# A second wave of projections made steps of the fill, its first wave evicted from PSUM, and the roots of the norms on ScalarE, in a two-layer hybrid encoder on one core

## The chip, the core and the metric

The kernel runs on one core of one Trainium2 chip. The metric is the time of one execution on the device in microseconds. The engines are TensorE (PE in the profile, PEld its weight loads), VectorE (DVE), ScalarE (ACT), GpSimd (POOL) and SyncE (SP), which here issues nearly all DMAs.

## What is computed

1024 tokens of width 1024 pass through two layers, all in float32. Each layer has four groups of attention heads side by side, then an MLP. The part that the change touches, cut from the reference:

```python
h = rms_norm(x, norm1_g[l])                 # x * rsqrt(mean(x*x) + 1e-6) * g
proj = h @ w_in[l]
(a_cq, a_ckv, a_kr, b_q, b_k, b_v, c_q, c_k, c_v, d_q, d_k, d_v) = split(proj)
y_a = mla_mixer(a_cq, a_ckv, a_kr, ...)     # rms_norm of a_cq (192) and a_ckv (128), then up-projections
y_b = diff_mixer(b_q, b_k, b_v, ...)        # softmax(q1 k1) - lam * softmax(q2 k2), rope on q and k
y_c = swa_mixer(c_q, c_k, c_v, ...)         # window of 128, sink logits
y_d = na_mixer(d_q, d_k, d_v, rpb[l])       # neighbourhood on a 64-wide grid
mix = concat([rms_norm(y_a), y_b, rms_norm(y_c), rms_norm(y_d)])
x = x + mix @ w_out[l]
h = rms_norm(x, norm2_g[l])
x = x + square(relu(h @ w_up[l])) @ w_down[l]
```

After both layers stands one more RMSNorm.

## The kernel before

**Data.** x is held in SBUF channel by channel, 8 tiles of 128 x 1024 tokens. To keep float32 accuracy on TensorE each operand is split into a high and a low part (`split`: ScalarE copies the high part, VectorE or GpSimd subtracts), and each product takes three matmuls (`passes`, L220 to L222: high by high, low by high, high by low). A projection tile is 128 output channels: 8 blocks of the contraction x 3 passes x 2 halves of 512 tokens = 48 matmuls, each half into one PSUM bank.

**Banks.** During attention the eight PSUM banks are named `mm` (2), `tr` (2), `sb` (3) and `pv` (1): projections, transposes, scores, and probabilities times values.

**Start of a layer.** `attention` first runs a wave of three projection tiles (B's first Q, K and V tile: BQ[0], BK[0], BV[0]) through `several` on the six banks sb, sb, sb, tr, tr, pv, interleaved, while the norm of x is computed (`squares`, `rstd_cols`, `spread_here`; the factor 1/rms ends up in `rb`, one row for each token spread over all partitions, and in the cosine and sine tables `tabc` and `tabs`). ScalarE then copies each bank into an SBUF tile `raw` (L449, shown as `p<-sb`, `p<-tr`, `p<-pv`), and VectorE evicts from that copy: for Q and K `ev_rope` (three products with the tables, an add, and the split into a tile `both`, which is stored to DRAM as `qb` or `kb`), for V a product with `rb`, a transpose on TensorE into `tr` and the split (`to_values`, stored as `vb`). A second wave runs the same for BQ[1], BK[1], BV[1] on the same six banks, its additions and subtractions on GpSimd (`self.eng`). `part` tiles have three buffers and `both` tiles two, so an eviction needs the store before last to have landed.

**Attention with fill.** `weave` alternates steps of an attention (`main`) with single steps of a generator of other work (`fill`), by a ratio: with RB = (7, 8) eight steps of fill come for seven of B's attention. LB is the priority lead that the scheduler gives the main steps. During B's attention (`attn_b`: loads of `stack` and `v` tiles from qb, kb, vb; scores in `softmax`, L804; their row maximum on VectorE, L806, which also moves the scores from the bank to SBUF; exponential on ScalarE, L809; the factor `cb` between the two softmaxes, L890 and L891; transposes L840; products with v, L828 and L829) the fill is `proj_latent` and then `proj_d`. `one` is a projection tile of the fill: two halves, each through an `mm` bank and then its eviction. `proj_latent` makes A's latents, stored to DRAM as `lat`, and their norms: sums of squares `sq` of 128x8, then `rsqrt_cols`, `rows_of` (to DRAM, shown as `drows`). During D's attention the fill is `proj_c` and `latent_up`, which loads the latents as `latp`, into buffers that the projections leave, and projects them up (L720 and L220 to L222).

**Roots.** `rsqrt_cols` (L241 to L252) computes 1/sqrt on VectorE: a guess from the bits (L247), then three Newton rounds of three ops (L249, L188, L251). It is called 20 times. The line number L188 is that of the helper `tt`, so all tensor-tensor ops on VectorE and GpSimd show it and are told apart by their tiles. L194 and L198 are in `split`.

**Order.** The scheduler of the tile framework turns all this into one fixed list of instructions for each engine, by a timeline of its own and by the leads. On the chip each engine, and each queue of DMA issues, takes its list strictly in order and waits at semaphores.

## Time and profile before

| | |
|---|---|
| median of 3 runs | 2735.67 us (2726.91 to 2736.3) |
| the profiled execution, its own time | 2728.97 us |
| its span from first to last instruction | 2727.2 us |
| mean granted clock of TensorE | 0.967 |
| TensorE busy | 2553.1 us |
| VectorE, ScalarE, GpSimd busy | 1994.1, 1430.9, 1134.5 us |

A span has two layers. In layer 0, B's first tiles are projected up to 83 us, B's attention runs to 333, D's starts near 333, the last projection ends at 363, the MLP begins near 758; layer 1 begins near 1372. A row of waits names the engine and the line that waited, the releaser, the total in us, the times and the longest. A row of groups has line, engine, operation, tiles out<-in with sizes, the count, busy time and mean ns of one, then the idle time ahead of them with its releaser. A row of a timeline has start and length in us.

### The profile page before, as it was taken

To read this page: it belongs to the slowest core of one execution; us is meant where nothing else is said; L and a number is where in the kernel's file an instruction comes from. 1 tells how busy PE (TensorE), PEld (TensorE's weight loads), DVE (VectorE), ACT (ScalarE), POOL (GpSimd) and SP (SyncE) were. 2 spreads that over 40 slices of the span, in tenths; PEclk is the share of its full clock that TensorE was granted. 3 is DMA by queue.
4 is the path that set the end of the run, shared out by engine and by line. 5 is a ranking of instruction groups with operands and counts; after the bars stand their busy time and mean duration, and the time that the engine had idled before them with its cause. 6 is when DMAs were issued, how large, how long until landed. Compare 5 with 4: busy or idle time off the path is not lost.

```text
span 2727.2 us, 37613 instructions
## 1 busy us (share of the span) xinstructions
PE 2553.1 (94%) x12298; PEld 2110.1 (77%) x12298; DVE 1994.1 (73%) x3544; ACT 1430.9 (52%) x2547; POOL 1134.5 (42%) x754
## 2 busy tenths in 40 slices
PE   8989988899989999999999899889998999999997
PEld 6778876787778887888877688767886788878886
DVE  7787767674966669787567778677749666687786
ACT  4667757563534444444436676576635344444444
POOL 2555642111245554445435556331013455545552
...
GB/s 175 166 105 126 154 280 241 83 93 40 65 130 156 151 160 267 156 138 142 98 133 138 95 134 157 300 215 71 76 70 44 154 159 149 223 222 150 131 100 62
DMA packets 190516, 389.20 MB, mean 143 GB/s; under 512 B 23712, under 2 KB 30832, under 8 KB 190320
## 3 DMA queue, kind: packets, MB, share of 16 engines
q1 hardware_dynamic: 176496, 361.62, 43.0%
...
q14 instruction: 98, 0.80, 0.1%
...
## 4 chain that ended last, share of the span: by engine, by line
PE 70%; DVE 14%; DMA 7%; ACT 4%; issue 3%; SPq 1%; POOL 1%; DVEq 0%; ACTq 0%; POOLq 0%
PE u L220 8%; PE u L222 8%; PE u L221 8%; PE mm L220 5%; PE mm L221 5%; PE mm L222 5%; PE p L220 5%; PE p L221 5%; PE p L222 5%; PE sb L804 3%; PE tr L840 2%; DVE p L806 2%; DVE part L188 2%; PE pv L829 2%; PE pv L828 2%
## 5 line engine op out<-in xcount | busy, mean ns | idle before, releaser
L188 POOL TENSOR_TENSOR wl<-raw,wh 128x512 fp32r<-128x512 f32 x448 | 635.1, 1418 | 705.2 <-ACT wh L194 690.1
L194 ACT ACTIVATE wh<-raw 128x512 fp32r<-128x512 f32 x448 | 281.5, 629 | 579.8 <-PE u L221 315.0
L188 POOL TENSOR_TENSOR wl<-ws,wh 128x512 fp32r<-128x512 f32 (+1 forms) x112 | 148.1, 1325 | 456.9 <-ACT wh L194 426.0
L220 PE MATMUL u<-far,wh 128*128 128x512 f32 x768 | 301.5, 393 | 11.5 <-ACT ev L1237 8.3
L188 DVE TENSOR_TENSOR raw<-raw 128x512 f32<-128x512 f32 x256 | 226.4, 890 | 107.4 <-POOL wl L188 56.9
L222 PE MATMUL u<-far,wl 128*128 128x512 f32 x768 | 300.5, 391 | 1.9 <-POOL wl L188 1.9
L221 PE MATMUL u<-far,wh 128*128 128x512 f32 x768 | 300.3, 391 | 0.0
L188 DVE TENSOR_TENSOR ptl<-tr,pth 128x512 fp32r<-128x512 f32 (+2 forms) x384 | 238.3, 628 | 66.6 <-ACT pth L194 64.9
L809 ACT ACTIVATE p<-p,nm 128x1024 f32<-128x1024 f32 x192 | 220.1, 1147 | 99.8 <-DVE nm L806 98.9
L194 ACT ACTIVATE pth<-tr 128x512 fp32r<-128x512 f32 (+2 forms) x384 | 205.6, 546 | 121.0 <-PE tr L840 64.8
L220 PE MATMUL p<-far,wh 128*128 128x512 f32 x640 | 251.7, 393 | 7.6 <-DVE ev L188 7.6
L222 PE MATMUL p<-far,wl 128*128 128x512 f32 x640 | 250.9, 392 | 1.5 <-POOL wl L188 1.5
L221 PE MATMUL p<-far,wh 128*128 128x512 f32 x640 | 251.0, 392 | 0.0
L804 PE MATMUL sb<-stack 96*128 96x512 f32 x640 | 218.5, 424 | 24.7 <-DVE nm L806 24.0
L188 DVE TENSOR_TENSOR far<-act,far 128x512 fp32r<-128x512 f32 x224 | 208.6, 960 | 14.6 <-ACT far L194 14.6
L188 POOL TENSOR_TENSOR p<-p 128x1024 f32<-128x1024 f32 x64 | 154.3, 2415 | 141.1 <-ACT p L893 125.0
L220 PEld LDWEIGHTS u<-far,wh 128*128 128x128 f32 x768 | 145.4, 189 | 43.6 <-ACT ev L1237 9.2
L222 PEld LDWEIGHTS u<-far,wl 128*128 128x128 f32 x768 | 145.0, 189 | 33.2 <-POOL wl L188 2.7
L220 PE MATMUL mm<-xh,wh 128*128 128x512 f32 x416 | 169.4, 407 | 0.8 <-DVE rows L272 0.2
L806 DVE CUSTOM_DVE_ANT_0 p<-sb,zero,nm 128x512 f32<-128x512 f32 x192 | 142.4, 743 | 36.3 <-PE sb L804 32.8
L221 PEld LDWEIGHTS u<-far,wh 128*128 128x128 f32 x768 | 145.3, 189 | 30.2
L221 PE MATMUL mm<-xl,wh 128*128 128x512 f32 x416 | 166.6, 400 | 0.0
...
## 6 DMA issues: line engine op xcount, KB each, us to landing
act<-acts SPq DMA_DIRECT2D x224, 256.0 KB
raw<-in_w_up SPq DMA_DIRECT2D x128, 256.0 KB
acts<-ev SPq DMA_DIRECT2D x128, 256.0 KB
raw<-in_w_down SPq DMA_DIRECT2D x128, 256.0 KB
...
```

Of the source, the lines that this page charges most:

```text
L188: (eng or self.nc.vector).tensor_tensor(out=out, in0=a, in1=b, op=op)
L194: nc.scalar.activation(hi, src, AF.Copy)
L220: mm(ps, w[0], x[0][:, sl], start=start, stop=False)
L221: mm(ps, w[0], x[1][:, sl], start=False, stop=False)
L222: mm(ps, w[1], x[0][:, sl], start=False, stop=stop)
L804: self.nc.tensor.matmul(ps, q[:, qt * P:(qt + 1) * P], k[:, sl], start=i == 0, stop=i == len(passes) - 1)
L806: self.nc.vector.tensor_tensor_reduce(out=p[:, sl], in0=ps, in1=self.zero[:, 0:1].bitcast(F).broadcast_to([P, 512]), scale=-scale, scalar= ...
L809: self.nc.scalar.activation(p, p, AF.Exp, bias=nm[:, 1:2], scale=-1.0, accum_out=z)
L828: nc.tensor.matmul(out, v[:, kt], h[:, sl], start=kt == 0, stop=False)
L829: nc.tensor.matmul(out, v[:, kt], lo[:, sl], start=False, stop=kt == 7)
L840: nc.tensor.transpose(t[:, k * 256 + i * P:k * 256 + (i + 1) * P], p[:, (j * 2 + k) * P:(j * 2 + k + 1) * P], self.ident)
```

## The change

1. Only the first wave is left (`FIRST`). Its six banks are evicted by VectorE straight from PSUM; ScalarE's copies L449 go. V's transposes of the first tile go to `tr`, as before.
2. BQ[1], BK[1], BV[1] become `proj_b`, three `one` tiles on the two `mm` banks ahead of the rest of the fill of B's attention, evicted from PSUM, with additions and splits on GpSimd as for the second wave before; V's transposes of this tile now use `mm`. RB goes from (7, 8) to (3, 4). Per pass this makes 512 instead of 416 matmuls into `mm`, 48 instead of 96 into `sb`, 32 instead of 64 into `tr` and 16 instead of 32 into `pv`.
3. `rsqrt_cols` takes sums of squares, from PSUM where they are made there, and computes exp(-0.5 ln(ss / count + eps)) on ScalarE, its square on ScalarE, and one Newton round: `ms` and two ops on VectorE.
4. The norms of the two latents are joined in one call of 128x16 (18 calls in all), after one product that scales the sum of the 128-wide latent by 192/128; their rows are stored together. `spread` reads rows that lie one behind the other.
5. L891 becomes a TENSOR_SCALAR with two columns as factors. A load of ScalarE's function table for logarithm and exponential stands at the start of the program; the list of ScalarE has one such load before and one after.

ScalarE's list goes from 2325 to 2355 rows, VectorE's from 3546 to 3381, SyncE's from 1337 to 1335; GpSimd keeps 759.

```diff
-    def rsqrt_cols(self, ms):
+    def rsqrt_cols(self, ss, count):
+
         nc = self.nc
-        n = ms.shape[1]
-        r = self.cp.tile([P, n], F, tag="rs_r", name="rs_r")
-        t = self.cp.tile([P, n], F, tag="rs_t", name="rs_t")
-        nc.vector.tensor_scalar(r.bitcast(I32), ms.bitcast(I32), -0.5, 1597463007.0, ALU.mult, ALU.add)
-        for _ in range(3):
-            nc.vector.scalar_tensor_tensor(out=t, in0=r, scalar=-0.5, in1=r, op0=ALU.mult, op1=ALU.mult)
-            self.tt(t, t, ms)
-            nc.vector.scalar_tensor_tensor(out=r, in0=t, scalar=1.5, in1=r, op0=ALU.add, op1=ALU.mult)
+        n = ss.shape[1]
+        tile = lambda tag: self.cp.tile([P, n], F, tag=tag, name=tag)
+        ms, r, t = tile("ms"), tile("rs_r"), tile("rs_t")
+        nc.scalar.activation(r, ss, AF.Ln, scale=1.0 / count, bias=self.eps)
+        nc.vector.tensor_scalar(ms, ss, -0.5 / count, -0.5 * EPS, ALU.mult, ALU.add)
+        nc.scalar.activation(r, r, AF.Exp, scale=-0.5)
+        nc.scalar.activation(t, r, AF.Square)
+        self.tt(t, t, ms)
+        nc.vector.scalar_tensor_tensor(out=r, in0=t, scalar=1.5, in1=r, op0=ALU.add, op1=ALU.mult)
         return r
...
         for t in range(n):
-            nc.tensor.matmul(ps[:, t * g:(t + 1) * g], sq[:, t * P:(t + 1) * P], rhs, start=True, stop=True)
-        ms = self.cp.tile([P, n * g], F, tag="ms", name="ms")
-        nc.vector.tensor_scalar(ms, ps, 1.0 / count, EPS, ALU.mult, ALU.add)
-        return self.rsqrt_cols(ms)
+            nc.tensor.matmul(ps.rearrange("p (g t) -> p t g", g=g)[:, t], sq[:, t * P:(t + 1) * P], rhs,
+                             start=True, stop=True)
+        return self.rsqrt_cols(ps, count)
     def rows_of(self, col, grid=False):
...
     def spread(self, dst, rows, j=0, g=1):
-        src = rows.rearrange("(t g) p -> g t p", g=g)[j]
-        n = dst.shape[0]
-        self.load(dst.rearrange("p (t q) -> p t q", t=8), src.partition_broadcast(n))
+        src = rows.rearrange("(g t) p -> g (t p)", g=g)[j]
+        self.load(dst, src.partition_broadcast(dst.shape[0]))
     def spread_here(self, dst, col):
...
         ka, va = dr([2, 2, P, S], "kan"), dr([4, P, 8, P], "va")
-        def evacs_b(t):
+        def evacs_b(t, tag="mm"):
             return [self.ev_rope(tabs, qb[:, t]), self.ev_rope(tabs, kb[:, t]),
-                    self.ev_plain(rb, self.to_values(vb[2 * t:2 * t + 2], "tr"))]
+                    self.ev_plain(rb, self.to_values(vb[2 * t:2 * t + 2], tag))]
         def one(t, xs, ev):
...
                     xs = self.normed(self.g1[:, l], lambda n: self.big_tile(R, n))
-                    def wave():
-                        return [(self.bank(a), self.bank(b)) for a, b in (("sb", "sb"), ("sb", "tr"), ("tr", "pv"))]
-
-                    banks = wave()
+                    banks = [(self.bank(a), self.bank(b)) for a, b in (("sb", "sb"), ("sb", "tr"), ("tr", "pv"))]
                     self.several(first, xs, banks, ahead)
                     acc = self.squares(self.x, self.ap, "p", self.NP)
                     with tc.high_priority(offset=200):
                         self.spread_here(rb, self.rstd_cols(acc, DM, self.ones[:, 0:1]))
                     tabs = self.table("32", rb, nc.vector)
                     self.eng = nc.vector
-                    for t in range(2):
-                        for ev, b in zip(evacs_b(t), banks):
-                            raw = self.ptile()
-                            for n in range(2):
-                                sl = slice(n * 512, n * 512 + 512)
-                                nc.scalar.activation(raw[:, sl], b[n], AF.Copy)
-                                ev(n, raw[:, sl])
-                        if t == 0:
-                            banks = wave()
-                            self.several([w_in(t) for t in self.WAVES[1]], xs, banks)
-                        self.eng = nc.gpsimd
-
-                    fill = chain(self.proj_latent(l, one, xs, rb, tabs, lat, krd, rows), proj_d())
+                    for ev, b in zip(evacs_b(0, "tr"), banks):
+                        for n in range(2):
+                            ev(n, b[n])
+                    self.eng = nc.gpsimd
+
+                    def proj_b():
+                        for t, ev in zip((T_BQ[1], T_BK[1], T_BV[1]), evacs_b(1)):
+                            yield from one(t, xs, ev)
+
+                    fill = chain(proj_b(), self.proj_latent(l, one, xs, rb, tabs, lat, krd, rows), proj_d())
                     self.weave(chain.from_iterable(self.attn_b(l, t, qb, kb, vb, y["b"]) for t in range(2)),
...
     EARLY, RC, RA, LA = 4, (8, 1), (3, 1), 0
-    WAVES = [(T_BQ[t], T_BK[t], T_BV[t]) for t in range(2)]
-    NP, RB, RD, LB, LD = 6, (7, 8), (3, 2), 40, 50
+    FIRST = T_BQ[0], T_BK[0], T_BV[0]
+    NP, RB, RD, LB, LD = 6, (3, 4), (3, 2), 40, 50
     def weave(self, main, fill=iter(()), ratio=(1, 0), lead=0, end=True, every=1):
...
         nc = self.nc
-        squares = [self.col("sq%d" % i, 8) for i in range(3)]
+        cols = self.col("sq", 24)
+        both = cols[:, 0:16]
+        squares = [cols[:, i * 8:i * 8 + 8] for i in (0, 2, 1)]
         for i, t, g in ((0, T_CQ, self.gq[:, l, 0:1]), (2, T_CKV, self.gkv[:, l:l + 1])):
...
         self.tt(q, q, squares[1], ALU.add)
-        for m, count in ((q, 192), (k, 128)):
-            nc.vector.tensor_scalar(m, m, 1.0 / count, EPS, ALU.mult, ALU.add)
-            rows_out.append(self.rows_of(self.rsqrt_cols(m)))
+
+        nc.vector.tensor_scalar(k, k, 192 / 128, None, ALU.mult)
+        rows_out.append(self.rows_of(self.rsqrt_cols(both, 192)))
         yield True
     def latent_up(self, l, lat, rows, qa, ka, va):
         nc, d = self.nc, self.d
         rq, rkv = self.big_tile(F, "rq"), self.big_tile(F, "rkv")
-        self.spread(rq, rows[0])
-        self.spread(rkv, rows[1])
+        self.spread(rq, rows[0], 0, 2)
+        self.spread(rkv, rows[0], 1, 2)
         parts = []
...
                 nc.vector.reciprocal(c, z[1][:, qt:qt + 1])
-                nc.vector.scalar_tensor_tensor(out=c, in0=z[0][:, qt:qt + 1], scalar=self.nlam[:, l:l + 1], in1=c,
-                                               op0=ALU.mult, op1=ALU.mult)
+                nc.vector.tensor_scalar(c, c, z[0][:, qt:qt + 1], self.nlam[:, l:l + 1], ALU.mult, ALU.mult)
                 nc.scalar.activation(ps[1], ps[1], AF.Copy, scale=c)
```

How the lists of the engines move, at the three places that the prediction speaks of.

**TensorE behind the first wave of layer 0.** `xh` and `xl` are the high and low parts of x times the norm's gain, `wh` and `wl` those of a weight block; the first operand named is the bank. Before, behind the first wave, from the second wave on:

```order
L638 MATMUL tr<-ident,part 128x128 x8
L222 MATMUL sb<-xh_177,wl 128x512 x2
L220 MATMUL sb<-xh_181,wh 128x512
L221 MATMUL sb<-xl_182,wh 128x512
L222 MATMUL sb<-xh_181,wl 128x512
L220 MATMUL sb<-xh_181,wh 128x512
L221 MATMUL sb<-xl_182,wh 128x512
L222 MATMUL sb<-xh_181,wl 128x512
```

The changed kernel at the same place:

```order
L224 MATMUL mm<-xh_188,wl 128x512
L222 MATMUL mm<-xh_192,wh 128x512
L223 MATMUL mm<-xl_193,wh 128x512
L224 MATMUL mm<-xh_192,wl 128x512
L636 MATMUL tr<-ident,part 128x128 x8
L222 MATMUL mm<-xh_164,wh 128x512
L223 MATMUL mm<-xl_165,wh 128x512
L224 MATMUL mm<-xh_164,wl 128x512
```

Ahead of V's transposes TensorE now has one tile, BQ[1], in the two mm banks, where six banks were being filled; the next tile needs an mm bank that VectorE has evicted.

**VectorE at the evictions of the first two B tiles of layer 0.** `both<-tr` is the split of V behind its transposes. Before:

```order
L188 TENSOR_TENSOR part<-p,rb 128x512 x2
L188 TENSOR_TENSOR both<-part,both 128x512
L188 TENSOR_TENSOR both<-tr,both 128x8x64 x2
L188 TENSOR_TENSOR part<-p,tabc 128x512
L188 TENSOR_TENSOR part<-p,tabs 64x512 x2
```

The changed kernel:

```order
L190 TENSOR_TENSOR part<-tr,rb 128x512
L190 TENSOR_TENSOR part<-pv,rb 128x512
L190 TENSOR_TENSOR both<-part,both 128x512
L190 TENSOR_TENSOR part<-mm,tabc 128x512
L190 TENSOR_TENSOR part<-mm,tabs 64x512 x2
L190 TENSOR_TENSOR part<-mm,tabc 128x512
L190 TENSOR_TENSOR both<-tr,both 128x8x64
L190 TENSOR_TENSOR part<-mm,tabs 64x512 x2
L190 TENSOR_TENSOR both<-tr,both 128x8x64
L190 TENSOR_TENSOR part<-mm,tabc 128x512
L806 ISA p,nm<-sb,zero 128x512
```

The evictions of BQ[1] stand around V's splits, and the first row maxima of B's scores (L806) follow a little later, between those of BK[1]. On SyncE's list nine loads of `stack` tiles, which wait for K's stores, stand in the changed kernel between the last K store and the store of V's first half; before, one load of a stack stood there.

**VectorE at the roots of the latents of layer 0.** Before, in part:

```order
L688 TENSOR_SCALAR sq_829<-sq_829 128x8
L806 ISA p,nm<-sb,zero,nm 128x512
L806 ISA nm 128x1
L247 TENSOR_SCALAR rs_r<-sq_829 128x8
L247 TENSOR_SCALAR rs_r<-sq_831 128x8
L249 SCALAR_TENSOR_TENSOR rs_t<-rs_r 128x8 x2
L188 TENSOR_TENSOR rs_t<-rs_t,sq_829 128x8
L188 TENSOR_TENSOR rs_t<-rs_t,sq_831 128x8
L251 SCALAR_TENSOR_TENSOR rs_r<-rs_t,rs_r 128x8 x2
L249 SCALAR_TENSOR_TENSOR rs_t<-rs_r 128x8 x2
L198 SCALAR_TENSOR_TENSOR both<-part,par,both 64x512
L188 TENSOR_TENSOR rs_t<-rs_t,sq_829 128x8
```

The changed kernel:

```order
L251 TENSOR_SCALAR ms<-sq 128x16
L806 ISA p,nm<-sb,zero 128x512
L806 ISA nm 128x1
L200 SCALAR_TENSOR_TENSOR both<-part,par,both 64x512
L806 ISA p,nm<-sb,zero,nm 128x512
L806 ISA nm 128x1
L890 RECIPROCAL cb<-z_1123 128x1
L891 TENSOR_SCALAR cb<-cb,z_1122,nlam 128x1
L190 TENSOR_TENSOR rs_t<-rs_t,ms 128x16
L255 SCALAR_TENSOR_TENSOR rs_r<-rs_t,rs_r 128x16
L806 ISA p,nm<-sb,zero 128x512
L806 ISA nm 128x1
```

Two interleaved chains of small ops become one, with row maxima (L806) between its ops. Before B's first scores TensorE's list has 54 us of work at full clock in place of 68, by the counts of rows and the pace of 0.23 us of a matmul.

10 lines of the change are left out of this document (8 added, 2 removed).

## The prediction

> **What bounds the kernel now.** I read the engine shares first, to see whose time the span is.
>
> ```profile
> PE 2553.1 (94%) x12298; PEld 2110.1 (77%) x12298; DVE 1994.1 (73%) x3544; ACT 1430.9 (52%) x2547; POOL 1134.5 (42%) x754
> ```
>
> TensorE is busy for 94% of the span, and the change leaves its list of matmuls all but as it was. So the change can only win what TensorE loses: 6% idle time, and stretches at a lower granted clock. Where these losses lie is read from the table of stages. The first number is the length of the stretch, then come the busy times of PE, PEld, DVE, ACT and POOL, then the granted clock and the DMA share.
>
> ```profile
> 45.80:83.20 37.40, 34.53 (x153) 27.61 (x152) 24.45 (x28) 9.97 (x18) 12.41 (x9) 1.00 0.76 201
> 83.20:106.90 23.70, 19.39 (x71) 15.12 (x70) 21.30 (x36) 13.42 (x22) 14.62 (x10) 0.78 0.73 227
> 106.90:150.80 43.90, 43.00 (x241) 35.92 (x240) 35.09 (x94) 34.78 (x57) 22.53 (x13) 1.00 0.38 109
> 150.80:188.80 38.00, 28.02 (x129) 22.08 (x128) 32.78 (x83) 22.54 (x35) 22.82 (x12) 0.78 0.31 84
> 188.80:363.40 174.60, 173.97 (x963) 148.76 (x962) 128.78 (x340) 126.45 (x216) 96.09 (x56) 1.00 0.55 155
> 363.40:387.30 23.90, 16.30 (x84) 14.03 (x83) 14.05 (x34) 9.90 (x24) 13.28 (x8) 0.86 1.04 291
> 387.30:438.30 51.00, 42.71 (x240) 34.61 (x239) 41.79 (x109) 37.35 (x97) 12.70 (x9) 0.97 0.90 284
> 1417.00:1457.00 40.00, 36.28 (x143) 28.27 (x141) 29.57 (x49) 19.58 (x33) 26.25 (x17) 0.87 0.79 232
> 1482.00:1525.00 43.00, 34.34 (x182) 27.73 (x180) 39.94 (x94) 27.60 (x45) 26.63 (x16) 0.83 0.44 117
> ```
>
> Busy time times granted clock is the work at full clock; the length less that is what a stretch loses. In layer 0 the second wave (45.8 to 83.2) loses 37.4 - 34.5 = 2.9 us, the start of B's attention (83.2 to 106.9) 23.7 - 19.39 x 0.78 = 8.6, the next stretch 0.9, the stretch from 150.8 16.1, the 175 us behind it 0.6. Then the stretch of D's attention with the first latent up-projections (363.4 to 387.3) loses 23.9 - 16.30 x 0.86 = 9.9 and the one after it 9.6. So 28.5 us are lost from the second wave to 188.8, and 19.5 us early in D's attention. Layer 1 repeats this: its two rows lose 40.0 - 36.28 x 0.87 = 8.4 and 43.0 - 34.34 x 0.83 = 14.5. What ends TensorE's idle time is in the tables of waits: first from 30 to 220 us, then from 330 to 400, then from 1380 to 1570.
>
> ```profile
> PE sb L804 <- DVE nm L806: 10.9, 7, 5.0
> ```
>
> ```profile
> PE mm L720 <- DMA latp<-lat: 2.7, 2, 2.2
> PE mm L221 <- DMA latp<-lat: 2.4, 1, 2.4
> PE mm L220 <- DMA latp<-lat: 1.3, 1, 1.3
> ```
>
> ```profile
> PE sb L804 <- DVE nm L806: 10.6, 8, 5.7
> ```
>
> In both layers B's scores wait for VectorE's row maxima (L806), and early in D's attention the latent up-projections wait 6.4 us for a load.
>
> **Part 1: the second wave becomes fill, evicted from PSUM.** Its matmuls stay, only later and in other banks. ScalarE's copies go, and VectorE's operands come from PSUM.
>
> ```profile
> L449 ACT ACTIVATE p<-sb 128x512 f32<-128x512 f32 x12 | 6.9, 590 | 26.0 <-PE sb L222 26.0
> L188 DVE TENSOR_TENSOR part<-p,tabs 64x512 f32<-64x512 f32 x32 | 39.8, 1244 | 2.8 <-POOL part L188 2.4
> L188 DVE TENSOR_TENSOR part<-mm,tabs 64x512 f32<-64x512 f32 (+1 forms) x40 | 27.6, 689 | 0.7
> ```
>
> Per layer 12 copies of about 0.59 us leave ScalarE (7.1 us), and 16 VectorE products with the sine table fall from 1.24 to 0.69 us (8.9 us). That work lies beside TensorE, so it counts only where TensorE waits for it. Against it stands what the second wave covered: TensorE ran 144 matmuls in six banks while VectorE evicted the first wave and while its values made their round trip.
>
> ```profile
> 61.31 0.68 DVE L188 TENSOR_TENSOR both<-part,both 128x512 fp32r<-128x512 f32 x1
> 64.83 0.69 DVE L188 TENSOR_TENSOR both<-tr,both 128x512 fp32r<-128x512 f32 x1 [2.84 <-ACT both L642]
> 68.74 0.69 DVE L188 TENSOR_TENSOR both<-tr,both 128x512 fp32r<-128x512 f32 x1 [3.22 <-ACT both L642]
> ```
>
> ```profile
> L642 ACT ACTIVATE both<-tr 128x512 fp32r<-128x512 f32 x8 | 4.8, 596 | 15.9 <-DMA kb<-both 15.7 <-PE sb L804 0.2
> ```
>
> Here the new wait lies. The split of V into the two `both` buffers waits for the stores of K (15.7 us of ScalarE's waiting over both layers), and VectorE waits behind it, 2.84 and 3.22 us. Afterwards the evictions of BQ[1] and BK[1] are queued behind that split on VectorE, and they alone free the two mm banks. Walking the changed order with the durations above, I find TensorE idle some 8 to 9 us up to the first scores, against 2.9 + 8.6 = 11.5 lost in before by 106.9. The walk can't see the clock or when stores land, so I take a **gain of 0** for the start, between a loss of 8 (a second round of those store waits, 2.84 + 3.22, with some clock lost) and a gain of 8 (nearly all of the 8.6).
>
> **Part 2: B's attention up to 188.8, with the joined latent root.** The worst gap there, on VectorE, GpSimd and TensorE in turn:
>
> ```profile
> 163.87 1.92 DVE L688 TENSOR_SCALAR sq<-sq 128x8 f32<-128x8 f32 x1
> 166.37 1.79 DVE L247 TENSOR_SCALAR rs_r<-sq 128x8 int32<-128x8 int32 x2
> 168.12 2.34 DVE L249 SCALAR_TENSOR_TENSOR rs_t<-rs_r 128x8 f32<-128x8 f32 x2
> 170.42 1.32 DVE L188 TENSOR_TENSOR rs_t<-rs_t,sq 128x8 f32<-128x8 f32 x2
> ```
>
> ```profile
> 163.40 2.35 POOL L188 TENSOR_TENSOR tabc<-tabc,rb 128x1024 f32<-128x1024 f32 x1
> 165.72 2.33 POOL L188 TENSOR_TENSOR tabs<-tabs,rb 128x1024 f32<-128x1024 f32 x1
> 168.02 2.34 POOL L188 TENSOR_TENSOR p<-p 128x1024 f32<-128x1024 f32 x1
> ```
>
> ```profile
> 173.63 0.80 PE L804 MATMUL sb<-stack 96*128 96x512 f32 x1 [4.98 <-DVE nm L806]
> ```
>
> Ops of 8 columns last as long as the GpSimd op beside them: VectorE's ends at 165.79, 168.16 and 170.46 stand within about 0.1 us of GpSimd's 165.75, 168.05 and 170.36. Meanwhile no row maximum is taken, and a score waits 4.98 us for its bank. The change replaces these two roots (two TENSOR_SCALARs ahead, then 10 ops each) by one chain with four VectorE ops and three on ScalarE, spread among the softmax ops, so I expect this gap to go. What is late next: VectorE itself. It is busy 32.78 of these 38 us, and the evictions of the second tile of B, done by 106.9 before, now fall partly into this stretch. Counting rows by durations for the same TensorE work (about 58 us of it), VectorE had 63 us in before with 27 in the last third, and has 66 afterwards, spread evenly. So I take half of the 16.1 us, **8 us per layer**, between -4 (the 3 us of added VectorE work on the path) and 16.
>
> Two small groups of VectorE go with this part.
>
> ```profile
> L891 DVE SCALAR_TENSOR_TENSOR cb<-z,nlam,cb 128x1 f32<-128x1 f32 x64 | 28.6, 447 | 1.2
> L890 DVE RECIPROCAL cb<-z 128x1 f32<-128x1 f32 x64 | 10.2, 159 | 17.6 <-ACT p L809 17.4
> L688 DVE TENSOR_SCALAR sq<-sq 128x8 f32<-128x8 f32 x4 | 4.5, 1134 | 0.1
> ```
>
> L891 becomes a TENSOR_SCALAR. At L890's price it saves 64 x (447 - 159) = 18 us of VectorE; at that of L688, a TENSOR_SCALAR too, it costs 64 x (1134 - 447) = 44 more. It has one column like L890, so I take the saving. Most of it falls where TensorE has no idle time (0.6 us in 175), so it adds nothing to the sum beyond the 8 us; the other end is in the -4.
>
> The Trainium skill, "SBUF — State Buffer", section "Who interferes with whom", says that a VectorE instruction with two SBUF inputs, or one such as tensor_scalar in a two-port mode, shuts out GpSimd or is shut out for a whole instruction, while one with a single SBUF input outside these modes is not. The rows agree for L249 and for the products, 1244 ns from SBUF and 689 from PSUM; by the same rule L891's new form may still be delayed, as L688 is, and the 8 us would be about 0 if all 64 were.
>
> **Part 3: the early part of D's attention.** With the second wave in the fill and the ratio (3,4) in place of (7,8), 192 of 768 projection matmuls are left at B's last score, by the two listings, where 74 of 624 were. D's first score comes after 253 us of TensorE work instead of 281, and 48 instead of 30 of the scores of D and C stand ahead of the first latp matmul; from the release of the buffers of the projections to that matmul lie about 11 us of TensorE work in place of 8.3. That covers 2.7 of the 6.4 us of waiting on latp, and part of the loss of clock (0.86): **5 us per layer**, between -3 (the share of DMA is 1.04 there, and a denser start loads more at once) and 10, which is half of the 19.5.
>
> **Part 4: the other roots.**
>
> ```profile
> PE mm L297 <- DVE rs_r L251: 4.8, 1, 4.8
> ```
>
> ```profile
> 753.46 0.15 DVE L263 TENSOR_SCALAR ms<-mm 128x8 f32<-128x8 f32 x1
> 758.18 0.17 DVE L251 SCALAR_TENSOR_TENSOR rs_r<-rs_t,rs_r 128x8 f32<-128x8 f32 x1
> ```
>
> ```profile
> 2713.68 0.16 DVE L263 TENSOR_SCALAR ms<-u 128x4 f32<-128x4 f32 x1 [1.96 <-PE u L261]
> 2715.65 0.16 DVE L251 SCALAR_TENSOR_TENSOR rs_r<-rs_t,rs_r 128x4 f32<-128x4 f32 x1
> ```
>
> ```profile
> L352 ACT ACTIVATE lam_e<-lam_e 128x2 f32<-128x2 f32 x2 | 0.4, 192 | 1.3 <-DVE lam_e L351 1.3
> ```
>
> Ahead of the MLP the chain from L263 to the last L251 takes 758.35 - 753.46 = 4.9 us with other VectorE ops between, and TensorE waits 4.8. Three ScalarE ops of about 0.19 us and two of VectorE of 0.17, with a few of those others still between, make about 2.9: **2 us** in layer 0, and I take **1.5** for the same chain in layer 1. The chain at the end takes 2715.81 - 2713.68 = 2.1 us, and three of 0.19 plus two of 0.16 with some room for changes of engine make 1.2: **0.9 us**. The bounds of the three are 0 and 6 together. The roots of the sub-norms and group norms lie beside full TensorE stretches: nothing, and 2 us each if uncovered. The functions of the new roots need a table on ScalarE, which is loaded once:
>
> ```profile
> 0.73 1.28 ACT L194 ACT_TABLE_LOAD   x1 [0.73 <-PEq L1479]
> ```
>
> The changed listing holds one load too, so I charge nothing.
>
> **The sum**, against the profiled execution's own 2728.97 us: 2 x (0 + 8 + 5) + 2 + 1.5 + 0.9 = 30.4, so 2698.6. That execution is 6.7 us below the median of the runs shown, 2735.67; with half of this difference added I predict **2702 us**.
>
> **The rivals.**
> - *The start gets slower.* The K stores take long (the DMA share is 0.76 and 0.73 there), and V's first store now stands on SyncE's queue behind nine loads of stacks. VectorE stands in the V split while two full mm banks stop TensorE, where six banks ran on before. Price: the 7.9 us of store waits per layer, in the open for both tiles' `both` pair, and a clock loss like today's first 8.6: some 17 us per layer, 34 in all, less 4 from the roots, so about 2759. It decides if a store lands later than about 9 us after its issue. For it: the 3.22 us waits exist already. Against it: the kernel before lost 8.6 us there too.
> - *Nothing comes of it.* The second wave's 144 matmuls only change places, the gap at 173.63 is taken over by VectorE's evictions, and 175 us of full TensorE show that the fill has no idle time to use. Roots alone: 2728.97 - 4.4 = 2725; with some loss at the start, 2733.
> - *Both stalls vanish.* 8.6 + 16.1 per layer, 10 from D's two stretches and 4.4 from roots: 2728.97 - 63.8 = 2665. For it: the evictions from PSUM escape GpSimd. Against it: VectorE's 66 us of work for 58 of TensorE's.
>
> **How the numbers follow.** The forecast with its own range of 2684 to 2720 has 0.45, the larger gain 0.13, no change 0.20, slower 0.22. About 0.5% (13.7 us) is what a measurement of this kernel can tell from no change: faster is below 2722, slower above 2749. Faster takes the first two, 0.58; the slower rival gives 0.21 to slower, and 0.21 is left within. The range leaves out the lower half of the larger gain and the upper half of the slower case: **2664 to 2758**.
>
> **What would show it.** Right: no score waits over 2 us for L806 near 170 us; L891's mean near 0.16 us; a loss up to the first 82 us of TensorE work like today's; waits on latp near 4 us; about 3 us at the MLP's root. Wrong: waits of the mm banks' matmuls on VectorE of over 4 us between 55 and 80 us with a clock below 0.8 (the slower case), or VectorE near 100% from 130 to 190 us with the score waits as long as before (no change).

## The result, and the profile after

**Same time.** Over 12 runs of each on one chip the changed kernel has a median of 2732.49 us (2723.7 to 2744.56), the kernel before 2732.3 (2725.18 to 2740.56): a ratio of 1.0003 with a 95% interval of 0.9986 to 1.002. Forecast were 2702 us and a range from 2664 to 2758. So the time lies within the range, but the gain of 30 us that was forecast isn't there. The engine shares of the changed kernel hardly differ on TensorE; VectorE has 61 us less.

```profile
PE 2553.6 (94%) x12296; PEld 2110.7 (77%) x12296; DVE 1932.7 (71%) x3379; ACT 1429.7 (52%) x2577; POOL 1129.1 (41%) x754
```

The table of stages, at cuts of the changed kernel itself (the waves' end, the first scores, the latents' root, B's end at 305, the last projection at 372), has length, then busy times of PE, PEld, DVE, ACT, POOL, then clock and DMA share:

```profile
46.10:73.00 26.90, 22.62 (x93) 18.01 (x92) 20.70 (x27) 5.40 (x9) 7.74 (x6) 0.87 0.69 196
73.00:96.50 23.50, 21.34 (x96) 16.32 (x96) 15.83 (x41) 15.40 (x26) 17.32 (x12) 1.00 0.92 282
96.50:152.80 56.30, 53.31 (x292) 43.49 (x291) 42.19 (x117) 43.53 (x71) 24.08 (x12) 0.97 0.33 105
152.80:183.20 30.40, 27.97 (x137) 22.45 (x135) 25.62 (x58) 22.86 (x39) 22.28 (x13) 0.89 0.37 105
183.20:305.20 122.00, 117.51 (x644) 100.41 (x644) 91.85 (x242) 88.01 (x142) 65.80 (x36) 0.97 0.40 120
305.20:371.60 66.40, 64.76 (x348) 55.31 (x347) 36.20 (x88) 35.54 (x82) 30.75 (x22) 1.00 0.74 202
371.60:400.00 28.40, 22.38 (x117) 18.96 (x116) 17.89 (x40) 13.54 (x35) 11.85 (x8) 0.88 1.01 280
400.00:441.90 41.90, 28.07 (x144) 22.59 (x142) 27.00 (x69) 24.04 (x61) 11.61 (x8) 0.84 0.93 290
```

With busy time times clock as work, the first four stretches lose 7.2 (26.9 - 22.62 x 0.87), 2.2, 4.6 and 5.5 us, together 19.5 in place of the 28.5 before. That looks like a gain of 9 us, but the cut at 183.2 us falls into the middle of the wait for the latents' root: from 183.2 to 188.7 TensorE is busy for 3.11 us at a clock of 0.50, which loses another 3.9 us. So about 23 us stand against 28.5, and the count of matmuls below leaves still less of the gain in layer 0. B's second half loses 122 - 117.51 x 0.97 = 8.0, those 3.9 among them, where the 175 us from 188.8 lost 0.6 before. The stretch from 400 loses 41.9 - 28.07 x 0.84 = 18.3; that is the largest loss of the table.

The waits of TensorE name the place. First those for VectorE at the start of B, layer 0 from 30 to 220 us and layer 1 from 1372 to 1560; then, from 365 to 490 us and from 1715 to 1845, a wait that stood at 3.2 and 3.4 us before:

```profile
PE sb L804 <- DVE nm L806: 6.9, 9, 2.4
PE mm L222 <- DVE part L190: 2.7, 2, 1.8
PE tr L636 <- DVE part L190: 2.4, 1, 2.4
```

```profile
PE sb L804 <- DVE nm L806: 3.7, 7, 1.0
PE mm L222 <- DVE part L190: 2.2, 1, 2.2
...
PE tr L636 <- DVE part L190: 1.8, 1, 1.8
```

```profile
PE pv L1026 <- DVE y L190: 11.8, 5, 7.9
```

```profile
PE pv L1026 <- DVE y L190: 5.0, 4, 2.1
```

Scores wait for VectorE's row maxima 6.9 and 3.7 us in place of 10.9 and 10.4 in the same stretches, and in place of the single gap of 4.98 us the longest is 2.4, at 185.6 us, still beside the latents' root. The waits for VectorE's evictions (`part`) have grown, from 2.0 and 2.9 us to 5.1 and 4.0. What is new behind B is the wait of `pv` for `y`, up to 7.9 us at once. The timeline of the changed kernel shows its chain, engine by engine:

```profile
417.59 1.33 ACT L199 ACTIVATE mixh<-rz,g_sub 128x512 fp32r<-128x512 f32 x2 [4.33 <-DMA rz<-yb]
419.01 0.34 SPq L169 DMA_DIRECT2D yb<-y  x1
424.12 0.68 DVE L190 TENSOR_TENSOR y<-pv,pvt 64x512 f32<-64x512 f32 x1 [3.93 <-DMA yb<-y]
424.95 0.77 PE L1026 MATMUL pv<-zero 128*128 128x512 f32 x1 [7.88 <-DVE y L190]
```

B's last output `yb` is stored at 419 us; only when that store has landed is its `y` buffer free (there are two), VectorE can evict a pv bank into it, and TensorE gets the bank. VectorE's wait for the store is 3.9 of the 7.9 us; ahead of it VectorE stands in B's tail (`mixl`), whose load ScalarE waits for. In the kernel before the same store was issued earlier, although B ended 28 us later there:

```profile
406.22 0.34 SPq L167 DMA_DIRECT2D yb<-y  x1
```

The roots became what was expected of them. Ahead of the first MLP and at the end of the program, the first and the last op of each chain:

```profile
758.83 0.27 ACT L250 ACTIVATE rs_r<-mm,eps 128x8 f32<-128x8 f32 x1 [1.20 <-PE mm L265]
761.92 0.17 DVE L255 SCALAR_TENSOR_TENSOR rs_r<-rs_t,rs_r 128x8 f32<-128x8 f32 x1
...
2715.82 0.26 ACT L250 ACTIVATE rs_r<-u,eps 128x4 f32<-128x4 f32 x1 [1.12 <-PE u L265]
2716.79 0.16 DVE L255 SCALAR_TENSOR_TENSOR rs_r<-rs_t,rs_r 128x4 f32<-128x4 f32 x1
```

They take 762.09 - 758.83 = 3.3 us in place of 4.9, and 1.1 in place of 2.1.

**Times at equal work.** Each kernel has the same matmuls in another order, so times of milestones can't be compared directly. For the table below each matmul record counts as the pace of its size (from the kernel before's trace, such that 20% of the intervals between its start and the next start are shorter: 0.226 us for 512 columns, 0.118 for 256, 0.175 for 384, 0.029 for a transpose of 128); summed up, this is work, about 2263 us in each kernel. A cell says how many us a kernel gained (-) or lost (+) against the kernel before's first trace while it did that piece of work. A0 ends at 140 us of work (194 us in the kernel before), B0 at 240 (308.5), D0 at 380 (about 536), M0 at the end of layer 0's MLP (about 1356); A1, B1, D1 are the same pieces of layer 1, M1 the rest. Each row is one profiled execution; its sum lies within 12 us of what the medians give, so the columns, not the sums, are what they are for.

```
                        A0     B0     D0     M0     A1     B1     D1     M1    sum
before, again         -1.1   -0.0   +0.1   -1.6   -2.7   +0.1   +0.6   -1.7   -6.4
changed               -0.1   +4.1   +1.0   -0.1   -6.0   -0.8   +7.2   -4.1   +1.1
changed, again        -4.1   +3.9   +5.8   -1.6   -3.4   -0.7   +7.7   -4.6   +2.8
e1  move alone        +5.6   +1.9   -2.5   +0.1   +2.1   -2.5   +5.7   +0.3  +11.0
e2  roots alone       -6.8   +1.6   -6.9   -0.4  -11.3   +0.6   +4.6   -3.5  -22.1
e3  RB (1,2)         -10.4   +3.0   -0.2   -0.3  -14.2   +0.0   +9.1   -2.7  -15.3
e4  waves from PSUM   -3.0   +2.3   -5.6   +0.3   -5.7   +0.0   +8.6   -0.1   -3.1
e5  RB (1,1)          -0.1  +19.0   -0.3   -1.0   -3.0  +16.7   +4.3   -2.6  +32.9
e6  roots, e4        -11.7   +5.2   -7.4   -1.3  -15.3   -0.9   +7.8   -3.5  -27.1
e7  L891 alone        -1.7   +1.5   +4.6   -1.1   -2.6   -0.3  +14.0   +1.2  +15.5
e8  more DMA in D     +1.0   -0.1   -0.4   -0.9   -2.9   +0.1  +10.1   -1.2   +5.7
e11 RB (1,3)         -14.7  +10.6   +9.1   -0.5  -17.5   +7.0  +14.5   -3.6   +5.2
e12 roots, old L891   -3.4   +0.7   +1.8   -1.7   -4.8   -2.4   +8.7   -3.7   -4.6
e17 move, RB (1,2)    -0.6  +12.9   -6.4   +1.3   -5.4   +3.4  +17.2   +3.8  +26.2
e18 faster tails      -5.3   +4.1   -8.9   -0.3   -3.0   -2.7   -3.2   -2.7  -22.1
```

The second trace of each of the two kernels shows what a cell is worth: the same lists differ by up to 4.0 us, and once by 4.8, in D0. So -1.1 in A0 and -2.7 in A1 are what the kernel before gains on itself, and the changed kernel's -0.1 and -4.1, -6.0 and -3.4 are hardly more than that. B0 begins at 194 and D0 at 308.5 us of the kernel before, so D0 holds the last 25 us of B's attention. In D1 every changed program of the table but e18 loses 4 to 17 us, those without the moved wave too; a part of D1's +7 is then not particular to the move, and why the kernel before is so good there is open. Some of the profiled executions lie well off their kernel's median: e18's is 8.4 us below it, e3's 6.6 below, e11's 6.1 above.

### The profile page after: what moved, and what is told of

It is laid out like the page before. It is cut to its first block, busy times and chain, and to the rows that moved or that the text cites. A ratio compares the mean times of both kernels' runs of the same rounds, so it can differ in the third digit from the quotient of the medians.

```text
span 2728.4 us, 37493 instructions
## 1 busy us (share of the span) xinstructions
PE 2553.6 (94%) x12296; PEld 2110.7 (77%) x12296; DVE 1932.7 (71%) x3379; ACT 1429.7 (52%) x2577; POOL 1129.1 (41%) x754
## 5 line engine op out<-in xcount | busy, mean ns | idle before, releaser
L222 PE MATMUL mm<-xh,wh 128*128 128x512 f32 x512 | 207.4, 405 | 8.7 <-DVE part L190 7.2
L223 PE MATMUL mm<-xl,wh 128*128 128x512 f32 x512 | 204.8, 400 | 0.0
L224 PE MATMUL mm<-xh,wl 128*128 128x512 f32 x512 | 204.6, 400 | 0.0
L222 PEld LDWEIGHTS u<-far,wh 128*128 128x128 f32 x768 | 145.6, 190 | 43.0 <-ACT ev L1236 6.8
L840 PE MATMUL tr<-ident,p 128*128 128x128 f32 x1024 | 160.6, 277 | 9.8 <-POOL p L190 5.0
```

Of the source, the lines that this page charges most:

```text
L222: mm(ps, w[0], x[0][:, sl], start=start, stop=False)
L223: mm(ps, w[0], x[1][:, sl], start=False, stop=False)
L224: mm(ps, w[1], x[0][:, sl], start=False, stop=stop)
L840: nc.tensor.transpose(t[:, k * 256 + i * P:k * 256 + (i + 1) * P], p[:, (j * 2 + k) * P:(j * 2 + k + 1) * P], self.ident)
```

## The experiments

The theory (T, with F and Y as its parts) is that the parts do win time early in a layer, and that it is given back in B's second half, where the ratio leaves too little fill, and behind B, where something comes later. The rivals are that nothing was won at all (R), that the granted clock takes back what idle time goes (C), or that the DMA engines are the limit behind the projections (D). Ratios are to the kernel before on the same chip, with 95% intervals.

**e1 and e2: the two parts alone.** e1 is the changed kernel with the old `rsqrt_cols`, `rstd_cols`, `spread`, latent norms and L891; e2 is the kernel before with the new ones.

```diff
# e1, against the changed kernel: old rsqrt_cols, and so on
-        nc.scalar.activation(r, ss, AF.Ln, scale=1.0 / count, bias=self.eps)
+        for _ in range(3):
...
# e2, against the kernel before: the same lines the other way round, the two waves kept
```

> The changed kernel with the old roots, the old latent norms, the old way of spreading rows and the old L891: the moved wave alone. Theory T (the fill wins some 10 us per layer up to 190 us of a layer, but its 192 instead of 74 left-over projections end later, and D's and C's stretch, which is full of DMA, ends later by as much): 2735 to 2742, some 5 us above the changed kernel, because the roots' 5 us are missing. Rival R (the win at the start was never there and the roots alone hold the time): 2738 to 2745. Both say slower than or equal to before; they differ in the milestones: T wants B's first 32 scores about 15 us earlier than before.

> The kernel before with the new roots, the joined latent norms, the new spread and the new L891, its two waves and their copies as they were. T: the small ops that stood behind GpSimd near 165 us go, projections end where they ended before, so nothing is given back: 2712 to 2724, with 4 to 6 us of it at the MLPs' and the final root. Rival R (roots hide beside full TensorE; only the MLPs' and the final roots count): 2726 to 2729. Rival C (the granted clock takes back whatever idle time goes): 2730 to 2734.

Measured: e1 2744.46 us, 1.0058 (1.0039 to 1.0077); e2 2703.91 us, **0.9907** (0.9889 to 0.9925). Had the parts added, the changed kernel would be at 0.9965, 0.0038 below what it is; the three intervals together make an error of about 0.003, so this is just clear of it. e1 lies in R's range and above T's, though its first scores come early as T wanted; e2 is far below R's and C's ranges, and below T's too. So the roots' part wins more than any theory had for it. The waits of e2's TensorE for row maxima from 30 to 220 us are below those of before, with the longest still 4.5 us, at 167 us and beside the root:

```profile
PE sb L810 <- DVE nm L812: 7.8, 5, 4.5
```

In the table e2 wins 6.8 and 11.3 us by 140 us of work of a layer, 3.5 in M1; the moved wave alone loses 5.6 and 2.1 there, although its first 32 scores come at 124.8 us in place of 140.5. So the gain at the start comes with the roots' part, which holds L891's new form as well, and in e1 the move is a loss.

**e3, e5 and e11: how thick the fill is.**

```diff
-    NP, RB, RD, LB, LD = 6, (3, 4), (3, 2), 40, 50
+    NP, RB, RD, LB, LD = 6, (1, 2), (3, 2), 40, 50    # e5: (1, 1), e11: (1, 3)
```

> The changed kernel with the fill ratio RB = (1, 2) in place of (3, 4): more fill per step of B, so that by the order of TensorE's list the last projection comes after 303 us of work, not 312, and only some 50 instead of 192 of its 912 projection matmuls are left at B's last score. T: the last projection and the first latp matmul come 8 to 10 us earlier than in the changed kernel, the end of C's attention too, in both layers: 2710 to 2718. Rival C (the clock takes it back) or R: within 4 us of the changed kernel, 2729 to 2736. Rival D (the DMA-bound stretch behind the projections sets the time by its bytes alone and starts with B's end): slower, 2736 to 2745.

> The changed kernel with RB = (1, 1): thinner fill, 657 instead of 720 of 912 projection matmuls are through at B's last score by TensorE's list, the last projection comes after 314 us of work (312 in the changed kernel, 303 with (1, 2)). Theory F (B's steps wait for VectorE and ScalarE, and what matters is how much independent work TensorE has between them): slower than the changed kernel by 5 to 12 us, 2733 to 2740 where before is 2727.5, the loss between 100 and 250 us of a layer. Rival T (the end of the last projection sets the time behind it): the last projection hardly moves, so within 3 us of the changed kernel, 2725 to 2731.

> The changed kernel with RB = (1, 3), fill still thicker: last projection after 302 us of work (303 with (1, 2), 312 with (3, 4)). Theory F: what the ratio can win is won with (1, 2), since TensorE has no gaps left in B's second half: 2714 to 2724, within 4 us of (1, 2). If earlier projections are worth something by themselves (T): 2708 to 2716. If scores now come too late for VectorE and ScalarE to keep up with (64 of 128 scores after 204 us of work, 158 with (1, 2)): 2728 to 2740.

Measured: (1, 1) 2758.01 us, 1.0108 (1.0088 to 1.0128); (3, 4) as changed 1.0003; (1, 2) 2720.84 us, 0.9976 (0.9964 to 0.9988); (1, 3) 2728.55 us, 0.9998 (0.9988 to 1.0008). e3 lies between T's range and its rivals', e5 above both of its ranges, and e11 at the lower end of the range for scores that come too late. T's step that the last projection alone sets the time is out: (1, 1) moves it by 2 us of work and costs 28 us. But F as I put it, that thick enough is enough, is not borne out either: (1, 3) doesn't keep what (1, 2) wins. The table shows where: the thicker the fill, the more is won in A (-0.1, -10.4, -14.7 in A0 of e5, e3, e11) and the more is lost in B and D of e11 (+10.6 and +9.1), as would follow if fill that is spent early isn't there later. Too thin a fill loses in B itself (e5, +19.0 and +16.7). How e5 stands in B's middle, from 210 to 300 us, and the kernel before in the same stretch:

```profile
210.00:300.00 90.00, 84.99 (x443) 71.63 (x442) 63.44 (x157) 59.19 (x97) 43.25 (x23) 0.93 0.35 100
```

```profile
210.00:300.00 90.00, 89.70 (x501) 76.62 (x500) 70.91 (x194) 68.75 (x111) 45.60 (x26) 1.00 0.48 138
```

Five us of idle time (90 - 84.99) come with a granted clock of 0.93 in place of 1.00, so that 11 us of work (89.70 - 84.99 x 0.93) are missing.

**e4 and e6: the waves straight from PSUM.**

```diff
-                            raw = self.ptile()
                             for n in range(2):
-                                sl = slice(n * 512, n * 512 + 512)
-                                nc.scalar.activation(raw[:, sl], b[n], AF.Copy)
-                                ev(n, raw[:, sl])
+                                ev(n, b[n])
```

> The kernel before without ScalarE's copies of the two waves: both waves are evicted straight from PSUM by VectorE, in the same six banks. T: VectorE's evictions get shorter (689 instead of 1244 ns) but hold the banks until VectorE is through, so TensorE waits for banks in the second wave: 2728 to 2742. If the copies were the reason for the loss from 83 to 107 us (8.6 us per layer): 2715 to 2722.

> The new roots, joined latent norms and L891 with the two waves of the kernel before, both evicted straight from PSUM (no copies on ScalarE): the parts of the change without the move into the fill. If the parts add (roots alone 0.9907, two waves from PSUM 0.9986): 0.989 of before, 2694 to 2702 where before is 2727.5. If the loss that the roots take away is the same as that of the copies: 0.991, 2700 to 2706.

Measured: e4 2724.77 us, 0.9986 (0.9973 to 0.9999); e6 2704.5 us, 0.9905 (0.9888 to 0.9922). The copies were worth 3.0 and 5.7 us in A0 and A1 (1.1 and 2.7 of which a second trace of the kernel before shows as well), and with the roots 4.9 and 4.0 more than the roots alone; by the time e6 can't be told from e2. So eviction from PSUM, at least out of the waves' six banks, is not what costs the move its time. e2 and e6 are the fastest versions here, both without the moved wave.

**e7 and e12: L891.**

```diff
-                nc.vector.scalar_tensor_tensor(out=c, in0=z[0][:, qt:qt + 1], scalar=self.nlam[:, l:l + 1], in1=c,
-                                               op0=ALU.mult, op1=ALU.mult)
+                nc.vector.tensor_scalar(c, c, z[0][:, qt:qt + 1], self.nlam[:, l:l + 1], ALU.mult, ALU.mult)
```

e7 makes this edit alone in the kernel before; e12 is e2 without it.

> The kernel before with L891 alone changed to the TENSOR_SCALAR form; every engine's list keeps its order. Theory P (the op with two tensors in SBUF waits out GpSimd, 64 times per run, and ScalarE's scaling of p waits behind it, 20.1 us in the profile of before): L891's mean falls from 447 to about 270 ns and the time to 2715 to 2723. Rival J (the gain of the roots comes from the joined latent norms and the MLP's and final roots): 2725 to 2729.

> The roots alone on the kernel before, with L891 left as it was. L891 alone made the kernel 13 us slower. If that was a cost of the op itself, it is saved here: 2688 to 2696. If it came from the other order that the scheduler made of all lists (3886 lines of difference on TensorE), it is not: 2698 to 2712, and the roots' gain up to 190 us of a layer stands either way.

Measured: e7 2744.88 us, **1.0048** (1.0034 to 1.0062), slower; e12 2723.86 us, 0.9978 (0.9965 to 0.9991). The group of e7, and the scaling of p on ScalarE that waits for it:

```profile
L892 ACT ACTIVATE p<-p,cb 128x1024 f32<-128x1024 f32 x64 | 72.8, 1144 | 13.9 <-DVE cb L891 12.4 <-DVE cb L890 1.2
L891 DVE TENSOR_SCALAR cb<-cb,z,nlam 128x1 f32<-128x1 f32 x64 | 17.3, 270 | 1.0
```

The op's mean did get shorter, 270 ns in place of 447, and ScalarE waits 12.4 us for it in place of 20.1. But the mean hides two kinds of ops. Of the old form 44 took 203 to 245 ns and 20 took 412 to 2251; 18 of these 20 began while GpSimd was busy with a product, and none of the 44 did. Of the new form all 64 took 250 to 276 ns, 20 of them begun beside such a product. So the new form saves the long waits of 20 ops, and the other 44 got a little slower. A0 and A1 show -1.7 and -2.6, no more than the kernel before's second trace; the time is lost in D0 and D1 (+4.6, +14.0), where only the last few of a layer's 32 L891 run. e7 lies above both of its ranges, and e12 above both of its own. My expectation that the lists keep their order was wrong: in the traces TensorE's order differs from the kernel before's from 168 us on. With the roots the same edit is worth 19 us the other way (e12 to e2). So an edit of 64 ops of under half a us moves the time by -19 to +13 us, and as far as the traces show it does so through the lists behind it. Gains of that size say little on the op itself, and for any single pair of lists here the same caution holds; e2's gain is met again in e6 and, with 16 us, in e16 against e13. What the roots win up to 140 us of work depends on the lists too: -3.4 and -4.8 in e12, -6.8 and -11.3 in e2.

**e8: is the stretch behind B bound by DMA?**

```diff
+                            if 2 <= i < 10:
+                                self.keep(junk[i - 2], src[i % 2].rearrange("p a b -> p (a b)"))
```

> The kernel before with eight more transfers of 512 KB from DRAM to DRAM per layer (parts of vd into a tile that nobody reads), issued early in D's attention; nothing else is changed and the result is not touched. Theory D (from the last projection on the DMA engines are full, 280 GB/s at a share of 0.9 to 1.04, and set the pace of D's and C's stretch): 4.2 MB at 0.28 GB per ms is 15 us per layer, so 2747 to 2760. Rival L (the stretch waits for latencies and for TensorE's list, not for bytes): below 2735.

Measured: 2734.72 us, 1.0014 (1.0 to 1.0028), 4 us in place of 30. But the experiment missed its stretch. The trace has the 16 extra transfers issued from 301.9 to 308.5 us and from 1652.2 to 1658.6, while B's last steps still ran; from 305 to 320 us the DMA engines moved 302 to 393 GB/s in place of 36 to 179, and by 320 to 325 their share was down at 0.59. From 363 us on, where they are full, they moved the same bytes as before. So the extra bytes filled idle time of the DMA engines ahead of the stretch, and the question isn't answered by this run. D0 is unchanged (-0.4); D1 lost 10.1 although TensorE's matmuls ran in the kernel before's order; why is open. What does speak against the bytes as the pace is e18 below: it moves the same 389 MB as the changed kernel and is faster behind B.

**e9 and e10: second traces**, of the two kernels unchanged.

> The kernel before once more, for a second trace: how far do the times at equal TensorE work differ between two executions of the same lists? If the stages are as steady as the whole, every stage is within 3 us of the first trace; if D's and C's stretch is where executions differ, it alone moves by 4 us or more.

> The changed kernel once more, for the same purpose: the loss in the second half of B's attention of layer 0 (8 us between 183 and 305 us in the first trace) is there again under theory F (fill too thin), and is absent if it was an accident of one execution.

One time each, 2722.56 and 2731.87 us. The kernel before's stages are within 3 us of its first trace. The loss of the changed kernel in B0 (+3.9 after +4.1) and in D1 (+7.7 after +7.2) is there again, so these belong to its lists; D0 is a loss in both, of 1.0 and 5.8.

**e13 to e16: B's tail written out ahead of D**, in the kernel before, e1, the changed kernel and e2, to have all four over nearly one order behind B.

```diff
+                    self.drain()
                     self.tails.append(self.mix_b(mix, y["b"], self.gsub[:, l:l + 1]))
```

> The kernel before with the tail of B's attention (its sub-norm, the store and reload of yb) written out ahead of D's attention, so that the scheduler puts the last yb store ahead of the latp loads; by the lists 192 of 912 projection matmuls are then left at B's last score and D starts after 250 us of work, as in the changed kernel, but with the two waves. Theory Y (what the changed kernel loses behind B is the late yb store, for which VectorE and the next pv bank wait): no such loss, 2716 to 2730 where before is 2729. Theory T (the left-over projections themselves and the later latp loads cost it): 2738 to 2748.

> The moved wave alone (e1_fill_only) with B's tail ahead of D: its lists from D's first score on are nearly those of e13, so the difference to e13 is what the moved wave itself costs up to B's end. Theory F (too thin a fill at (3, 4)): 5 to 12 us above e13. If the cost of the move was only in D's and C's stretch: within 4 us of e13.

> The changed kernel with B's tail ahead of D. Theory Y: the waits of pv on VectorE's y (11.8 us in layer 0, 5.0 in layer 1) go: 2712 to 2724 where before is 2729. Theory T: the last projection comes after 317 us of work instead of 312 and latp after 323 instead of 316, so slower than the changed kernel: 2734 to 2744.

> The roots alone (e2_roots_only) with B's tail ahead of D. With e13 to e15 this makes a square of both parts over one order of D's and C's stretch: if the parts add there, e15 - e14 = e16 - e13, each -17 to -25 us (some 6 to 10 per layer at the latents' root and 4 to 6 at the MLPs and the end). If the roots' gain in e2 was luck of its lists, e16 - e13 is -8 or less in size.

Measured: e13 2780.82 us, 1.0188 (1.0164 to 1.0211); e14 2767.19, 1.0141 (1.0119 to 1.0162); e15 2748.15, 1.0072 (1.0052 to 1.0092); e16 2764.83, 1.0126 (1.0103 to 1.0148). All are slower: with the tail in one block each of them loses 23 to 37 us between 220 and 260 us of work, at B's end in layer 0, and wins only a part of it back. I didn't foresee that cost, and it can't stand for the late store; on what the store costs in all, these runs are inconclusive. On where it costs they are used under e18. As a square they tell something too. Ahead of B's end the move costs e14 against e13 2.5 and 8.2 us (A0, A1), the roots win e16 against e13 5.3 and 4.8. And over this order the two parts do add up in time: the move -13.6 us, the roots -16.0, both -32.7. The move alone is a gain here and a loss of 16 us in e1; by these two pairs its sign hangs on what the scheduler puts behind it.

**e17: the moved wave alone with (1, 2).**

```diff
-    NP, RB, RD, LB, LD = 6, (3, 4), (3, 2), 40, 50     # in e1
+    NP, RB, RD, LB, LD = 6, (1, 2), (3, 2), 40, 50
```

> The moved wave alone (e1_fill_only, old roots and old L891) with RB = (1, 2) in place of (3, 4). Theory F (the moved wave costs time up to B's end only because (3, 4) leaves too little fill between B's steps): at equal work it is at or ahead of the kernel before up to 280 us of work in layer 0, where e1 was 7 us behind, and the time falls from e1's 2744 to 2726 to 2736. Rival: the two mm banks and the stores of K cost it whatever the ratio: 2738 to 2748, 5 us behind before at 140 us of work.

Measured: 2750.82 us, 1.009 (1.0075 to 1.0105). Up to 140 us of work F holds, A0 and A1 are -0.6 and -5.4 in place of +5.6 and +2.1; but the time missed, and B0 lost 12.9. In both layers TensorE stands at the transposes of the latents' roots behind the old chain of 20 ops, from 220 to 365 us and from 1372 to 1560:

```profile
PE mm L272 <- DVE rs_r L253: 4.1, 1, 4.1
```

```profile
PE mm L272 <- DVE rs_r L253: 5.0, 1, 5.0
```

It may be that thicker fill brings this chain to where TensorE needs it sooner; with the new roots the same ratio gave 0.9976. That would be one concrete way in which the parts don't add, but no run changes the chain alone.

**e18: the tails twice as fast during D.**

```diff
-    EV = (.5, .5, .7, 1)
+    EV = (.5, 1, .7, 1)
```

> The changed kernel with the tails of finished heads ticked at every step of D's attention instead of every second one: B's last yb store then stands ahead of the latp loads on SyncE's list, without the block that e13 to e16 put at B's end. Theory Y: the waits of pv on VectorE's y go from 11.8 us in layer 0 to below 3, and of the 5 to 9 us per layer that the changed kernel loses behind B some half comes back: 2718 to 2727 where before is 2729. Rival: the loss moves to another wait, since latp comes after 320 us of work instead of 316: 2729 to 2742.

Measured: 2716.09 us, **0.9962** (0.9947 to 0.9976). B's last store now goes out at 377 us, not 419, and the waits of pv for y in the two stretches behind B (365 to 490, 1710 to 1840) fall from 11.8 to 3.8 and from 5.0 to 2.6:

```profile
376.81 0.33 SPq L169 DMA_DIRECT2D yb<-y  x1
```

```profile
PE pv L1026 <- DVE y L190: 3.8, 4, 1.9
```

```profile
PE pv L1026 <- DVE y L190: 2.6, 3, 2.1
```

D0 and D1 turn from +1.0 (+5.8) and +7.2 (+7.7) to -8.9 and -3.2, while A0 to B1 stay near what they were. So the loss behind B was had back by this one edit, 11 us by the ratios. The lists behind B differ in more than that store (the last latp projection comes after 362 us of work, not 348), so not all of it is shown to be the store's; and the same edit in the kernel before, which would tell a better pace of the tails in general from a repair of the move, was not run.

The count of work shows one place in particular. To get from 310 to 315 us of work of a layer, where C's first scores stand, the kernel before takes 13.0 us in layer 0 and 8.7 in layer 1, the changed kernel 24.1 and 21.9 (26.0 and 23.4 in its second trace), e1 22.2 and 22.3, e5 25.8 and 25.2. With thicker fill (e3, e11, e17) it is 7.2 to 10.3. And it goes when the tail alone is put elsewhere: from e1 to e14 it falls to 6.8 and 8.4, from the changed kernel to e15 to 6.4 and 8.2, to e18 to 7.2 and 10.9. So in both layers this hole of the thin ratios goes with B's tail standing there. (In the kernel before layer 0's 13.0 us fall to 6.9 with the tail ahead, in e13.) What it costs in all is less clear, since e14 and e15 pay elsewhere. In layer 0 of the changed kernel it shows as the 7.9 us for `y` and a wait for VectorE ahead of C's first scores, which itself waits in part for a load of C's mask:

```profile
411.97 1.65 PE L976 MATMUL sb<-stack 128*128 128x384 f32 x4 [4.58 <-DVE nb L1083]
```

In layer 1 it shows as the same wait (3.7 us at once) and one for an mm bank (4.5), and not as one for `y`; the rows are of 1715 to 1845 us:

```profile
PE mm L222 <- DVE both L190: 5.2, 2, 4.5
...
PE sb L976 <- DVE nb L1083: 4.8, 4, 3.7
```

## Why the prediction was wrong

- **Part 1, gain 0 between -8 and 8.** Right. By 80 us of work of a layer the changed kernel stands at 0.0 and -0.8 us in layer 0 and at -0.8 and -0.6 in layer 1 (its two traces), the kernel before's second trace at -1.5 and -0.8. The move's loss in e1 (5.6 and 2.1 us in A0 and A1) comes behind that, in Part 2's stretch, and isn't there with thicker fill (e17, e3); the ratio, which I priced only behind B, belongs in that term.
- **Part 2, 8 us per layer: too large.** From 80 to 140 us of work the changed kernel's traces gain 0.3 and 3.5 us in layer 0 and 5.3 and 3.0 in layer 1, about 3 in place of 8; of those in layer 1 the kernel before's second trace shows 2.0 as well. The 16.1 us were counted with a gap of 4.98 us that was to go; 1.2 and 2.4 of it stayed, and VectorE's evictions took a part. In e2 a gap of 4.5 us stayed too, and yet A0 and A1 win 6.8 and 11.3, since the slow stretch around the root ended some 6 us sooner in layer 0 (the clock is back at 1.00 from 175 us on, not 180). The root's ops can still last long beside GpSimd (the two TENSOR_SCALARs of 128x16 from `sq` took 835 and 1142 ns, the other sixteen of that line 146 to 175), but there are four VectorE ops where twenty-two stood, three of them here (a row holds one engine's op):

```profile
180.92 1.14 DVE L251 TENSOR_SCALAR ms<-sq 128x16 f32<-128x16 f32 x1
181.02 0.29 ACT L250 ACTIVATE rs_r<-sq,eps 128x16 f32<-128x16 f32 x1
...
185.86 0.18 DVE L190 TENSOR_TENSOR rs_t<-rs_t,ms 128x16 f32<-128x16 f32 x1
186.08 0.18 DVE L255 SCALAR_TENSOR_TENSOR rs_r<-rs_t,rs_r 128x16 f32<-128x16 f32 x1
```

- **B's second half, which the sum left at 0.** It lost 4 us in B0 in both traces, and had them back by 290 us of work (+0.9 and -3.4 us there). I had read the 175 us at full TensorE as a stretch that needs nothing; too thin a fill can break it (e5, +19.0), but that the ratio made these 4 us isn't shown: e3 with thicker fill has +3.0, and e6 without the move +5.2.
- **Part 3, 5 us per layer: this is the step that failed.** The waits on latp did fall, to 3.5 us, but the second trace of the kernel before has 4.3, and e2, without the move, 2.2; so the left-over projections are not shown to have covered them. And they were not only cover. D's steps tick B's tail: the tail's last store went out 13 us later though B ended 28 us earlier, and the place from 310 to 315 us of work, with C's first scores, got 11 to 15 us longer per layer. With the tail put elsewhere (e14, e15, e18) that place is short again. From 290 to 315, which takes in the latp waits as well, the changed kernel loses 6 to 9.5 us per layer; in place of -5 per layer the columns have +1.0 to +5.8 and +7.2 to +7.7. I had looked at what the moved steps wait for, not at what is paced by them. What else D1 lost stays open.
- **Part 4, 4.4 us.** Right by the chains, 1.6 us shorter ahead of the first MLP and 1.0 at the end. M0 and M1 hold -4.2 and -6.2 in the changed kernel's traces, but a second trace of the kernel before has -3.3 there, so the columns alone don't show it; e2 has -3.9.
- **The sum.** Against -16 us forecast up to B's end, the changed kernel's two traces have -2.8 and -4.3 (A0 to B1 added up); against -10 behind B, +8.2 and +13.5; against -4.4 for the roots, -4.2 and -6.2. The rival of no change had the time right, and a part of the mechanism: the gap at 173.63 shrank to 2.4 and 1.2 us, and TensorE's waits for VectorE's evictions grew by 3.1 and 1.1. But it saw nothing of the loss behind B, without which the time would not have stayed the same.

Of the five signs that I named for being right three came: a start like that of before, waits on latp of 3.5 us and 3.3 us at the MLP's root. One score wait of 2.4 us stood at the root, where I had asked for none over 2, and L891's mean was 269 ns. None of the five looks at C's first scores, so together they could not tell a gain from none.

L891 came out at 269 ns in the changed kernel, between my two ends; I took the one of L890, 159. By the rule of the Trainium skill's page "SBUF — State Buffer", section "Who interferes with whom", an op with one tensor in SBUF may still be held up in a two-port mode. The trace agrees for L251 from `sq`, 835 and 1142 ns, and shows no such wait for L891, whose 64 ops took 214 to 276 ns. Both ends of my price took the mean of 447 for the old form's usual length; its median was 219.

What is left open: which instructions of the lists behind B make the columns D0 and D1 differ by up to 20 us between kernels whose work there is the same. B's tail with its late store accounts for the 7.9 us wait of the changed kernel in layer 0; but e17's last store is as late (419 us) and its pv waits only 0.8 us for y, so a late store alone doesn't make the wait. e7's 14 us in D1 are not traced to one wait. Whether the full DMA engines lengthen the loads and stores that are waited for there was not tested.
